# Pool mixer in column halves, another order of the conditioning weights, and copies and squares on ScalarE, in a two-layer diffusion backbone

## The chip, the cores and the metric

One core of one Trainium2 chip runs the kernel. The metric is the device time of one launch in microseconds (us); a time of a kernel is the median of its runs.

## What is computed

512 latent tokens and 256 context tokens of width 1024 go through two layers. Layer 0 mixes tokens by pooling, layer 1 by attention, and each is followed by a squared-ReLU MLP. Cut to what matters here:

```python
sh1, sc1, gt1, sh2, sc2, gt2 = ada_mods(c, w_ada[i], b_ada[i])   # silu(c) @ w_ada + b, six parts of 1024
h = modulate(rms_norm(x, g_mix_pre[i]), sh1, sc1)                # h * (1 + sc1) + sh1
# layer 0: four groups of 256 columns, windows 2, 4, 8, 16 over the tokens
diff_g = mean over window of h_g - h_g
y = concat_g(diff_g @ w_pool[g]) * pool_scale
x = x + gt1 * rms_norm(y, g_mix_post[i])
m = square(relu(modulate(rms_norm(x, g_mlp_pre[i]), sh2, sc2) @ w_mlp_in[i])) @ w_mlp_out[i]
x = x + gt2 * rms_norm(m, g_mlp_post[i])
# the context tokens take the same steps with the conditioning of c_ctx
```

`w_ada` has 4 MB for each of the six parts of a layer. The kernel loads it in chunks of 1 MB.

## The kernel before

Tokens are six tiles of 128 rows (t = 0 to 3 latents, 4 and 5 context), columns eight tiles of 128 (k = 0 to 7); pool group g holds k = 2g and 2g+1. Every product is made of three, from a rounded operand and its remainder (hH and hL of the activations, wpH and wpL of the pool weights): a cast on ScalarE makes the first, a subtraction on VectorE the second.

The stretch before the first MLP, which the change rewrites, has these parts:

- `rows_a`, `rows_b`: the rows come in, their mean squares go through GpSimd (`rstd`), and VectorE scales them into `acc`.
- `mean_mm(k)` (L420, tile psm): TensorE multiplies the rows by a band matrix, which gives window mean minus row for one k, in a PSUM tile of pool psA (two tiles of two banks each). `mean_ev` (L434) copies two of the eight into SBUF (tile stage); the others stay in PSUM until `centred`.
- `ada_mm` (L225, tile psada): one or two chunks of w_ada against the conditioning columns; VectorE turns the result (L227), four small products with `sel` finish the turn (L232), and `ada_out` adds the bias (L243) and makes scale and minus-shift columns (L252, L247). Chunks come in the order of the table `landing`: SC1 and SH1 for k 0 to 3 (two chunks each), SC1 and SH1 for k 4, 5 and for k 6, 7 (one chunk each), GT1 (four), then SC2 and SH2 in the same pieces.
- `centred(k)`: scale and shift of the mean (L452 on ScalarE, L454 on VectorE), cast (L455) and remainder (L456) into hH, hL.
- `pool_weights`: w_pool times pool_scale (L469), then its cast and remainder (L126, L129).
- `pool_a(t)` (L480, tile pspool): all four groups of one token tile, 24 matmuls into one psA tile. `pool_ms` takes the mean squares, `pool_b` (L325) multiplies by the gate rows, which `gate_rows` (L302, L304) spreads from GT1 in two column halves; `norm_r` (L328) adds to the residual, `norm_s` and `norm_c` (L512, L514) normalise for the MLP.
- `turn0`, `mod0`: transposes (L378, tile psx), scale and shift (L388, L390), cast and remainder (L394, L395). `Inner.part` (L553, tile psin) then multiplies by the first 256 columns of w_mlp_in, block by block.

After that comes the MLP of layer 0: `Inner` for its second 256 columns (96 matmuls on tile units), then fourteen rounds of `Seven` (Strassen-like products, L672) with `out_mm`, `out_ev` (L768 and L760 to L780) between them. VectorE also works off the conditioning of later parts there, one `ada_sum` (L263 to L272) for each call of `ada_step`, and builds the sums that `Seven` needs (`sums`, L617 to L620).

What sets the order: each step is put on a list with a number (`st.at`), and the list is run sorted. A scheduler then lays out each engine's instructions by its own estimate; only what is marked with `keep_in_program_order` keeps its place. Engines and the DMA queue of SyncE (SP) run their lists strictly in order. A load is issued when its buffer is free: w_ada and w_pool share the four buffers of pool `rawe`, pool_scale and the MLP weights the three of `rawp`. A buffer of a two-chunk unit is free after its matmuls for the first chunk, and after the `sel` products for the second, since the turned rows are put into it.

## Time and profile before

| | us |
|---|---|
| three runs | 1188.82, 1192.07, 1192.59 |
| median | 1192.07 |
| the profiled execution | 1189.55 |
| its span, first to last instruction | 1187.8 |
| around the span | 1.75 |
| TensorE (PE) busy in the span | 1147.0 |
| VectorE (DVE) | 950.5 |
| ScalarE (ACT) | 624.1 |

Starts in rows of the trace are microseconds from the start of the span. In a row of the timeline stand the start, the length of the merged run, engine, line, operation, tiles written and read, sizes, the count, and in brackets how long the engine sat idle before it and what ended that. A plain fp32 matmul (psm, psada, psg) counts twice, any other once. In a row by windows stand the window, its length, the busy time and number of instructions of PE, weight loads, DVE, ACT and POOL (GpSimd), TensorE's granted clock, the share of the DMA engines and GB/s.

### The profile page before, as it was taken

The page shows a single profiled execution, that of the slowest core. Times are in us where ns is not written, and L with a number is a line of the kernel's source. Part 1 is how long each engine was busy: PE and PEld are TensorE (multiplying, and loading weights), DVE is VectorE, ACT ScalarE, POOL GpSimd, SP SyncE. Part 2 cuts the span into 40 slices and gives each one's busy share as a digit, 9 for nine tenths or more (in the row PEclk, how much of TensorE's full clock was granted, in tenths as well). Part 3 has the DMA queues.
Part 4 walks back from the last instruction along what each step waited for, and adds up shares of the span by engine and source line. Part 5 has one row for each costly group of instructions (what it writes and reads, how often), then busy time and mean ns, then how long its engine had stood idle before and what let it go on. Part 6 is the DMA issues. An engine that isn't in the chain of part 4 may idle for free.

```text
span 1187.8 us, 15989 instructions
## 1 busy us (share of the span) xinstructions
PE 1147.0 (97%) x6170; PEld 990.3 (83%) x6170; DVE 950.5 (80%) x1564; ACT 624.1 (53%) x1063; POOL 67.7 (6%) x120
## 2 busy tenths in 40 slices
PE   5899999999999999999999999999899999999997
PEld 3679789989899889988887889998888888888886
DVE  3787968889889888986587689978687788778876
ACT  4666435443445444544576378872676346435522
POOL 2030000000000000000142210001100000000001
PEclk9899999999999999999999999999999999999999
DMA  9984134443444443333431301105344133314312
GB/s 338 363 292 178 36 107 142 142 142 107 144 136 146 142 142 95 130 131 107 179 105 36 107 1 36 37 4 195 122 141 154 46 120 133 113 39 142 107 33 109
DMA packets 100011, 147.84 MB, mean 124 GB/s; under 512 B 2736, under 2 KB 75872, under 8 KB 99936
## 3 DMA queue, kind: packets, MB, share of 16 engines
q1 hardware_dynamic: 99936, 146.84, 36.6%
q8 instruction: 48, 0.79, 0.3%
q14 instruction: 27, 0.22, 0.1%
HBM read 139.49 MB, written 7.34 MB: 124 GB/s over the span
## 4 chain that ended last, share of the span: by engine, by line
PE 47%; issue 33%; DVE 9%; ACT 5%; POOL 3%; DMA 2%; SPq 0%; POOLq 0%; DVEq 0%; ACTq 0%
PE pso L768 19%; PE psin L672 17%; PE po L1226 2%; PE psq L1015 2%; PE pss L1187 2%; POOL rs L169 1%; DVE rows L268 1%; PE psin L553 1%; DMA raw<-in_w_mlp_in 1%; POOL rs L1024 1%; ACT junk L154 1%; DVE sm L1191 1%; PE psada L225 1%; PE pspt L1212 1%; DVE units L129 1%
## 5 line engine op out<-in xcount | busy, mean ns | idle before, releaser
L768 PE MATMUL pso<-units,rb 128*128 128x512 f32 x1152 | 279.7, 394 | 4.0 <-ACT pso L760 2.9
L768 PEld LDWEIGHTS pso<-units,rb 128*128 128x128 f32 x1152 | 215.7, 189 | 47.9 <-ACT pso L760 3.6
L268 DVE SCALAR_TENSOR_TENSOR rows<-raw,cond,rows 128x256 f32<-128x256 f32 x280 | 122.0, 477 | 0.7
L780 DVE TENSOR_TENSOR acc<-acc,pso 128x512 f32<-128x512 f32 x135 | 88.5, 676 | 31.6 <-PE pso L768 31.3
L553 PE MATMUL psin<-ra,rb 128*128 128x512 f32 (+1 forms) x432 | 104.8, 342 | 2.4 <-ACT ra L363 1.6
L872 PE MATMUL pso<-units,pairs 128*128 128x512 f32 x336 | 82.3, 389 | 0.0
L553 PEld LDWEIGHTS psin<-ra,rb 128*128 128x128 f32 x432 | 70.3, 189 | 13.6 <-ACT ra L363 1.9
L553 PE MATMUL psin<-ra 128*128 128x512 f32 x256 | 80.6, 389 | 0.0
L872 PEld LDWEIGHTS pso<-units,pairs 128*128 128x128 f32 x336 | 63.1, 188 | 13.1
L876 DVE TENSOR_TENSOR acc<-acc,pso 128x512 f32<-128x512 f32 x72 | 48.6, 681 | 27.6 <-PE pso L872 27.6
L167 POOL TENSOR_SCALAR ms<-ss 128x1 f32<-128x1 f32 x20 | 11.4, 572 | 1010.5 <-ACT junk L154 998.8
L672 PE MATMUL psin<-ra,units 128*128 128x384 f32 x336 | 66.0, 338 | 0.7 <-ACT psin L684 0.6
L672 PE MATMUL psin<-sums,units 128*128 128x384 f32 x336 | 63.7, 337 | 0.3 <-ACT units L638 0.2
L672 PEld LDWEIGHTS psin<-ra,units 128*128 128x128 f32 x336 | 59.3, 188 | 4.2 <-ACT psin L684 0.9
L129 DVE TENSOR_TENSOR units<-raw,units 128x1024 fp32r<-128x1024 f32 (+2 forms) x49 | 55.2, 1151 | 7.3 <-ACT units L126 7.1
L672 PEld LDWEIGHTS psin<-sums,units 128*128 128x128 f32 x336 | 58.8, 188 | 2.4 <-ACT psin L680 0.7
L760 ACT COPY pso<-acc 128x512 f32<-128x512 f32 x42 | 24.3, 589 | 67.2 <-DVE acc L780 65.2
L553 PEld LDWEIGHTS psin<-ra 128*128 128x128 f32 x256 | 48.0, 188 | 10.0
L126 ACT CAST units<-raw 128x1024 fp32r<-128x1024 f32 (+2 forms) x49 | 47.2, 995 | 14.3 <-PE pso L768 10.3
L553 PE MATMUL psin<-rb 128*128 128x512 f32 (+1 forms) x144 | 52.7, 367 | 0.2 <-DVE rb L364 0.2
L1015 PE MATMUL psq<-units,ra 128*128 128x512 f32 x216 | 51.7, 392 | 0.0
L553 PE MATMUL psin<-rb,ra 128*128 128x512 f32 x128 | 49.8, 389 | 0.0
(253 smaller groups left out, 2350.2 us busy)
## 6 DMA issues: line engine op xcount, KB each, us to landing
raw<-in_w_ada SPq DMA_DIRECT2D x48, 1024.0 KB, 5.4
raw<-in_w_mlp_in SPq DMA_DIRECT2D x32, 1024.0 KB, 5.4
raw<-in_w_mlp_out SPq DMA_DIRECT2D x32, 1024.0 KB, 5.1
raw<-in_w_qkv SPq DMA_DIRECT2D x6, 1024.0 KB, 5.3
spill<-xr SPq DMA_DIRECT2D x10, 512.0 KB, 9.3
xr<-spill SPq DMA_DIRECT2D x10, 512.0 KB, 5.9
raw<-in_w_o SPq DMA_DIRECT2D x4, 1024.0 KB, 5.4
xr<-in_x SPq DMA_DIRECT2D x4, 512.0 KB, 4.4
```

Source lines behind the costliest of these rows:

```text
L126: a = sc.copy(hi, raw)
L129: b = ve.tensor_tensor(out=lo, in0=raw, in1=hi, op=ALU.subtract)
L268: ve.scalar_tensor_tensor(out=r, in0=raw[:, k, :], scalar=cond[:, k, c:c + 1], in1=r, op0=ALU.mult, op1=ALU.add)
L553: te.matmul(ps[:, bank, o:o + ln], w[:, k, fs], rhs, start=start, stop=(k == KT - 1 and n == 2), skip_group_check=len(ks) < KT)
L672: te.matmul(bank, w[k], a[k], start=start and k == 0 and m == 0, stop=stop and k == 3 and m == 2, skip_group_check=True)
L760: sc.copy(ps, accv[:, t, c0:c0 + w])
L768: te.matmul(pss[h][:, 0:cols[h][1]], a[:, f, ts_], w[:, f, cols[h][0]:sum(cols[h])], start=(n == 0 and not seeded[t]), stop=(n == len(seq) ...
L780: ve.tensor_tensor(out=d, in0=d, in1=ps[:, 0:w], op=ALU.add)
L872: te.matmul(ps, a, w, start=(m == 0), stop=(m == len(seq) - 1))
L876: ve.tensor_tensor(out=M[n][:, t], in0=M[n][:, t], in1=ps, op=ALU.add)
L1015: te.matmul(ps, a[:, k, sl], w[:, k % 4, :], start=(k == 0 and n == 0), stop=(k == KT - 1 and n == 2))
L1187: te.matmul(ps[:, c2, 0:384], a[:, sl], b[:, kv, 384 * c2:384 * c2 + 384], start=(n == 0), stop=(n == 2))
```

## The change

- **Means.** `mean_mm` runs for all eight k in a row, one every 1.3 units of the list, and `mean_ev` copies every one into SBUF; `centred` then works there in place.
- **Chunk order.** In `landing` GT1 now comes third of four: SC1, SH1 for k 0 to 5, then GT1, then SC1, SH1 for k 6, 7, then SC2, SH2. The first matmul of each chunk and the turn on VectorE are kept in the order of the list.
- **Pool weights.** Loaded behind the first four chunks, and pool_scale right behind them, now also in pool `rawe`; multiplied and split in two halves.
- **Pool mixer by halves.** `pool_mm(t0, g)` does two token tiles for one group; a psA tile now holds one column half of two token tiles. Its gate, mean square and product follow for each half.
- **Rows by feature pair.** `norm_c`, `turn0` and `mod0` keep the normalised rows of two token tiles side by side for each k.
- **ScalarE.** In `Inner.square` of layer 0 the square is made in place by ScalarE and cast by it, and VectorE makes only the remainder; eight of the twelve copies of the first `out_ev` go to ScalarE.
- **Later conditioning.** `ada_step` is left out once (at g = 1), and what is due at the end is finished in `before0`.

```diff
@@ ada_mm
-                te.matmul(ps[q:q + 32, 0:w * P], cond[:, at, :], raw[:, k, :], start=(at < 4), stop=(at >= 4))
+                mm = te.matmul(ps[q:q + 32, 0:w * P], cond[:, at, :], raw[:, k, :], start=(at < 4), stop=(at >= 4))
+                if k == 0:
+                    tc.keep_in_program_order(mm)
-        ve.transpose(rows, ps[:, 0:w * P])
+        tc.keep_in_program_order(ve.transpose(rows, ps[:, 0:w * P]))
@@ mean_ev, centred
+            d = stage[-1][:, TOK * (k % 2):TOK * (k % 2) + TOK]
+        for z, ps, f in zip(d, means[k], (sc.copy, ve.tensor_copy)):
+            f(z, ps[:, 0:z.shape[-1]])
...
-                sc.activation(z, pm[ci][:, 0:ln], AF.Identity, scale=sa, bias=b)
+                sc.activation(z, z, AF.Identity, scale=sa, bias=b)
@@ pool weights
-        pscale = rawp.tile([P, 2048], F32, tag="raw", name="pscale")[:, 0:D]
-        sy.dma_start(pscale, pool_scale[0].partition_broadcast(P))
+        pscale = pools[0].tile([P, 2048], F32, tag="raw", name="pscale")[:, 0:D]
+        tc.keep_in_program_order(sy.dma_start(pscale, pool_scale[0].partition_broadcast(P)))
@@ pool mixer
-    def pool_a(t):
-        pp_ = psA.tile([P, 2, 512], F32, tag="a", name="pspool")
...
+    def pool_mm(t0, g):
+        if (t0, g // 2) not in pooled:
+            pooled[t0, g // 2] = psA.tile([P, 2, 512], F32, tag="a", name="pspool")
...
+    def pool_b(t, h):
+        gated(t, accv[:, t, :], pooled[t - t % 2, h][:, t % 2, :], 512 * h, 512 * h + 512)
@@ Inner.square
+            if self.ntok == TOK:
+                sc.activation(r, r, AF.Square)
+                sc.copy(hi[:, f, :], r)
+                ve.tensor_tensor(out=lo[:, f, :], in0=r, in1=hi[:, f, :], op=ALU.subtract)
+                return
@@ the list
-    landing = ((21, SC1, 0, 4), (26.3, SH1, 0, 4), (29, SC1, 2, 2), (32, SH1, 2, 2), (39, SC1, 3, 2), (42, SH1, 3, 2),
-               (47.3, GT1, 0, 4), (52.6, GT1, 2, 4), (61, SC2, 0, 4), (66, SH2, 0, 4),
+    landing = ((21, SC1, 0, 4), (26.7, SH1, 0, 4), (33.7, SC1, 2, 2), (36.5, SH1, 2, 2),
+               (42, GT1, 0, 4), (47.7, GT1, 2, 4), (50.5, SC1, 3, 2), (53.3, SH1, 3, 2), (61.7, SC2, 0, 4), (67.3, SH2, 0, 4),
...
+        st.at(15 + 1.3 * k, mean_mm, k)
@@ out_ev, extra0
-                ve.tensor_copy(d, ps)
+                (ve.tensor_copy if c0 and t % 3 else sc.copy)(d, ps)
...
-        if g:
+        if g > 1:
             ada_step()
```

**TensorE, from the first chunk of SC1 to the turn of SH1.** Tile psm is the window means, six matmuls for each k; psada from raw and cond is a chunk (four matmuls of 512 columns), psada from raw and sel a turn. Before, the rows from the means of k 2 on:

```order
L225 MATMUL psada<-raw,cond 32x512 x4
L420 MATMUL psm<-gate,acc 128x136
L420 MATMUL psm<-gate,acc 128x144 x2
L420 MATMUL psm<-gate,acc 128x136 x4
L420 MATMUL psm<-gate,acc 128x144 x2
L420 MATMUL psm<-gate,acc 128x136 x4
L420 MATMUL psm<-gate,acc 128x144 x2
L420 MATMUL psm<-gate,acc 128x136 x3
L225 MATMUL psada<-raw,cond 32x512 x12
L232 MATMUL psada<-raw,sel 32x2x4 x8
```

One chunk stood ahead of the means of k 2, 3 and 4, the three others of SC1 and SH1 behind them, and both turns at once behind these. Now, with the means of k 2, 3 and 4 already ahead of the first row shown:

```order
L225 MATMUL psada<-raw,cond 32x512 x8
L420 MATMUL psm<-gate,acc 128x136
L420 MATMUL psm<-gate,acc 128x144 x2
L420 MATMUL psm<-gate,acc 128x136 x4
L420 MATMUL psm<-gate,acc 128x144 x2
L420 MATMUL psm<-gate,acc 128x136 x3
L234 MATMUL psada<-raw,sel 32x2x4 x4
L420 MATMUL psm<-gate,acc 128x136
L420 MATMUL psm<-gate,acc 128x144 x2
L420 MATMUL psm<-gate,acc 128x136 x3
L225 MATMUL psada<-raw,cond 32x512 x8
L234 MATMUL psada<-raw,sel 32x2x4 x4
```

The two chunks of SC1 now stand behind the means of k 2 to 4, the turn of SC1 behind those of k 5 and 6, and the chunks of SH1 behind all eight.

**VectorE, the same place.** Before, from the copies of the first two means to the first centred column:

```order
L434 COPY stage<-psm 128x256 x2
L227 STREAM_TRANSPOSE raw<-psada 128x512
L970 TENSOR_SCALAR grow<-grow 128x128
L227 STREAM_TRANSPOSE raw<-psada 128x512
L243 TENSOR_TENSOR mods_92<-psada,cols 128x8
L252 SCALAR_TENSOR_TENSOR avec_94<-mods_92,cols 128x8
L243 TENSOR_TENSOR mods_92<-psada,cols 128x8
L247 TENSOR_SCALAR phase<-mods_92 128x8
L454 TENSOR_SCALAR work<-stage,avec_94,mods_92 128x256 x2
```

The two turns (L227) and the two sums of the mods (L243) stood close together. Now:

```order
L229 STREAM_TRANSPOSE raw<-psada 128x512
L435 COPY stage<-psm 128x256
L245 TENSOR_TENSOR mods_92<-psada,cols 128x8
L254 SCALAR_TENSOR_TENSOR avec_94<-mods_92,cols 128x8
L435 COPY work<-psm 128x256 x2
L474 TENSOR_TENSOR raw<-raw,pscale 128x1024 x2
L229 STREAM_TRANSPOSE raw<-psada 128x512
L129 TENSOR_TENSOR rb<-raw,rb 128x1024
L245 TENSOR_TENSOR mods_92<-psada,cols 128x8
L129 TENSOR_TENSOR rb<-raw,rb 128x1024
L249 TENSOR_SCALAR phase<-mods_92 128x8
L454 TENSOR_SCALAR stage<-stage,avec_94,mods_92 128x256 x4
```

The pool weights times pool_scale (L474, both halves) now stand ahead of the turn of SH1 (the second L229), and the first half's remainder (L129) ahead of its mods (the second L245).

**TensorE, the pool mixer and the gates.** Tile pspool is the mixer, psg the gate rows. Before, from the first pool matmul to the turn of the second half of GT1:

```order
L480 MATMUL pspool<-rb,ra 128x256 x17
L232 MATMUL psada<-rows,sel 32x2x2 x4
L225 MATMUL psada<-raw,cond 32x512 x4
L480 MATMUL pspool<-rb,ra 128x256
L225 MATMUL psada<-raw,cond 32x512 x4
L480 MATMUL pspool<-rb,ra 128x256 x22
L232 MATMUL psada<-raw,sel 32x2x4 x4
L480 MATMUL pspool<-rb,ra 128x256 x8
L302 MATMUL psg<-ident,gc 128x128 x8
L225 MATMUL psada<-raw,cond 32x512 x8
L232 MATMUL psada<-raw,sel 32x2x4 x4
```

All SC1 and SH1 chunks stood ahead of this place. Now:

```order
L488 MATMUL pspool<-rb,ra 128x256 x35
L234 MATMUL psada<-rows,sel 32x2x2 x4
L225 MATMUL psada<-raw,cond 32x256 x8
L488 MATMUL pspool<-rb,ra 128x256 x13
L225 MATMUL psada<-raw,cond 32x512 x8
L234 MATMUL psada<-rows,sel 32x2x2 x4
L234 MATMUL psada<-raw,sel 32x2x4 x4
L304 MATMUL psg<-ident,gc 128x128 x8
L488 MATMUL pspool<-rb,ra 128x256 x12
L225 MATMUL psada<-raw,cond 32x512 x8
L488 MATMUL pspool<-rb,ra 128x256 x24
L234 MATMUL psada<-raw,sel 32x2x4 x4
```

48 pool matmuls (left half of t 4, 5, 0 and 1) now stand ahead of the gates, with the chunk of SH1 for k 4, 5 and those of GT1 between them; the chunks for k 6 and 7 have moved behind the row that ends this piece. Further down, the mixer's right half waits for these, and on VectorE all six residual sums (L330) now stand behind the last `centred`.

138 lines of the change are left out of this document (71 added, 67 removed).

## Prediction, made before the changed kernel had run

> **What bounds the kernel now.** I read the stages first (busy time by windows), then the timeline of each engine in the stretch before the first MLP.
>
> ```profile
> 20.00:30.00 10.00, 8.23 (x89) 5.96 (x90) 2.74 (x9) 1.29 (x2) 0.00 (x0) 0.96 1.03 353
> 60.00:70.00 10.00, 10.00 (x84) 8.18 (x88) 8.72 (x9) 5.54 (x12) 2.73 (x6) 1.00 0.90 318
> 130.00:150.00 20.00, 16.68 (x74) 13.04 (x72) 20.00 (x35) 7.69 (x10) 0.00 (x0) 1.00 0.00 1
> 200.00:300.00 100.00, 100.00 (x508) 90.04 (x507) 90.86 (x177) 48.15 (x73) 0.00 (x0) 1.00 0.39 125
> ...
> 59.97 2.02 PE L302 MATMUL psg<-ident,gc 128*128 128x128 f32 x16 [0.58 <-DVE gc L291]
> 82.96 0.58 PE L553 MATMUL psin<-ra,rb 128*128 128x256 f32 x2
> 109.61 16.81 PE L553 MATMUL psin<-ra,units 128*128 128x384 f32 x96
> ```
>
> Early on the DMA engines are full (share 1.03) and TensorE waits now and then; from 60 on TensorE is full. The first stretch ends at 109.61, where the 96 matmuls of the second `Inner` begin. Behind it TensorE waits in one place only, 130 to 150 us, where VectorE is busy 20.00 of 20.00 us; from 200 on it has no gap. The matmuls are the same in number and kind in both kernels, so a full TensorE takes from the change neither gain nor loss. The change is worth what it does to 109.61, and to the wait behind it.
>
> **Step 1, to the turn of SC1 and the chunks of SH1.**
>
> ```profile
> 17.98 0.91 DVE L434 COPY stage<-psm 128x256 f32<-128x256 f32 x2 [1.21 <-ACT stage L434]
> 19.46 5.12 PE L420 MATMUL psm<-gate,acc 128*128 128x136 f32 x36
> 24.51 2.78 PE L225 MATMUL psada<-raw,cond 128*32 128x512 f32 x24
> 27.11 0.22 PE L232 MATMUL psada<-raw,sel 128*32 128x8 f32 x8
> 35.65 1.68 PE L420 MATMUL psm<-gate,acc 128*128 128x136 f32 x12
> 28.45 0.17 DVE L243 TENSOR_TENSOR mods<-psada,cols 128x8 f32<-128x8 f32 x1
> ...
> raw<-in_w_ada SPq DMA_DIRECT2D x48, 1024.0 KB, 5.4
> ...
> xr<-in_x SPq DMA_DIRECT2D x4, 512.0 KB, 4.4
> ...
> pscale<-in_pool_scale SPq DMA_DIRECT2D x1, 512.0 KB, 9.9
> ```
>
> Now the means of k 2 to 4 come first. The one for k 2 needs the first copy out of PSUM, about 18.5; three take 5.12, so 23.6. The two chunks of SC1 take 2 x 0.93 (2.78 for three): 25.5. The means of k 5 and 6 take 3.4, the turn 0.2 (0.22 for two): 29.1. Only now is the buffer free into which pool_scale goes, since it shares the four of `rawe`. Its load then takes 4.4, as 512 KB of x do: 33.5. (In the old place it shows 9.9 behind other loads, but here only w_pool is ahead; 9.9 is the upper end.) TensorE meanwhile does k 7 and the chunks of SH1, to 32.7, against 27.3 before. On SP's queue the next chunks stand behind pool_scale and the buffers of SH1, so SC1 for k 4, 5 is issued near 32 and lands at 37.5 (5.4); TensorE asks for it after the turn of SH1, at 37, and for the others later still, so this costs nothing. It is paid only if those turns come earlier.
>
> The Trainium skill, page "DMA: Bandwidth & Descriptors", section "Anatomy of one DMA — SWDGE (gpsimd) path", gives a DMA about 2.0 us and its bytes over 436 GB/s, an estimate of 3.2 us here; the row's 4.4 decides, and by the page the sum would be 1.2 us less.
>
> **Step 2, the shift of k 0 to 3.**
>
> ```profile
> 36.96 2.28 DVE L469 TENSOR_TENSOR raw<-raw,pscale 128x2048 f32<-128x2048 f32 x1
> 27.36 0.72 DVE L227 STREAM_TRANSPOSE raw<-psada 128x512 f32<-128x512 f32 x1 [0.89 <-PE psada L232]
> 41.21 2.29 DVE L129 TENSOR_TENSOR rb<-raw,rb 128x2048 fp32r<-128x2048 f32 x1 [1.17 <-ACT rb L126]
> 28.71 1.52 ACT L452 ACTIVATE work<-stage,mods,avec 128x512 f32<-128x512 f32 x2 [10.28 <-DVE mods L243]
> 30.80 3.13 ACT L455 ACTIVATE ra<-work,phase 128x256 fp32r<-128x256 f32 x6
> 44.35 3.80 PE L480 MATMUL pspool<-rb,ra 128*128 128x256 f32 x17 [0.18 <-DVE work L454]
> 62.91 6.01 PE L480 MATMUL pspool<-rb,ra 128*128 128x256 f32 x48
> ```
>
> VectorE runs in order, and the product with pool_scale stands ahead of the turn of SH1. So 33.5 + 2.28 + 0.72 for the turn + 1.14 for half a remainder + 0.2 = 37.8 for the mods of SH1, which were there at 28.6. ScalarE then does four L452 (3.0) and eight L455 (0.52 each, 4.2): 45.0. All of them now read SBUF in place of PSUM; the row shown (stage) does so already. The pool matmuls start after the first column, near 42.2; the first 17 took 3.80 after a pause, the other 18 take 2.25: 48.2. Before, they began at 44.35, held by the pool weights, so up to here little is lost.
>
> **Step 3, the gates.**
>
> ```profile
> 54.50 1.95 PE L302 MATMUL psg<-ident,gc 128*128 128x128 f32 x16
> 56.25 0.58 ACT L304 COPY gate<-psg 128x512 f32<-128x512 f32 x1
> L325 DVE TENSOR_TENSOR acc<-pspool,gate 128x512 f32<-128x512 f32 x12 | 7.7, 680 | 4.6 <-ACT gate L304 2.8 <-ACT junk L154 1.6
> ```
>
> TensorE next does a turn, the SH1 chunk, 13 pool matmuls, two chunks of GT1 and a turn (0.25 + 0.93 + 1.6 + 1.9 + 0.25): 53.1. Then it stands still: the turn of GT1 is behind three remainders of k 4 and 5 on VectorE, these behind ScalarE's L452 (1.5) and three L455 (1.6), these behind the mods that came at 53.3. So 56.5, remainder and turn 1.3, sel and gate columns 0.5: 58.3. Half the gate matmuls 1.0, a copy 0.58, two products of 0.68: 61.2. Only then is a psA tile free, because two halves of finished mixer (t 4, 5 and t 0, 1) hold both until their gate is there. A whole tile was held so before, too, but with the chunks for k 6 and 7 already done.
>
> **Step 4, the right half.** From 61.2 TensorE does 12 pool matmuls, two chunks and 24 pool matmuls (1.5 + 1.9 + 3.0): 67.6; turn and gate columns 0.7, gates 2.0, 12 pool matmuls 1.5: 71.8. Then SC1 for k 6, 7: chunk 0.93, transpose 0.44, turn 0.3, and the same for SH1: 75.1. Mods 0.3, two L452 and four L455 (1.5 + 2.1), the last remainder 0.5: 79.5. The first token tile's last matmuls take about 0.9: 80.4.
>
> ```profile
> 63.21 2.47 DVE L328 SCALAR_TENSOR_TENSOR xr<-acc,rs,xr 128x1024 f32<-128x1024 f32 x2
> L154 ACT ACTIVATE junk<-pspool 128x512 bf16<-128x512 f32 x12 | 7.1, 595 | 3.5 <-PE pspool L480 3.4
> 56.12 0.56 POOL L169 TENSOR_TENSOR rs<-ms,nhalf 128x1 f32<-128x1 f32 x1
> L328 DVE SCALAR_TENSOR_TENSOR xr<-acc,rs,xr 128x1024 f32<-128x1024 f32 x6 | 7.6, 1275 | 0.3
> L390 DVE TENSOR_SCALAR acc<-psx,avec,mods 128x256 f32<-128x256 f32 x12 | 6.1, 537 | 4.9 <-ACT acc L388 4.9
> L395 DVE TENSOR_TENSOR ra<-acc,ra 128x512 fp32r<-128x512 f32 x12 | 7.8, 687 | 1.0 <-ACT ra L394 1.0
> L514 DVE TENSOR_SCALAR acc<-xr,rs 128x1024 f32<-128x1024 f32 x3 | 2.3, 751 | 1.5 <-POOL rs L169 1.5
> ```
>
> Mean square 0.6, then GpSimd's two steps at 0.56 at most: the first residual sum at 82.1, where it was at 63.21. That is the heart of it: k 6 and 7 are due in the right half of all six tiles, and their chunks now come after the gates.
>
> **Step 5, VectorE's pile.** Between the first gated right half and the first remainder of the MLP's input, VectorE now has in one row six products (6 x 0.68), six residual sums (6 x 1.275), four quarters of w_mlp_in's remainder (4 x 0.69, as L395), three turns (0.72 each at most), three `norm_c` (3 x 0.75), three scalings (3 x 0.54) and five small ones (0.17 each): 21.3. The strided write of `norm_c` is not in the trace; at the price of the residual sum, 1.275, it adds 1.6, and less than 0.75 nothing suggests; I take 0.75, the same engine and size. From 81.0 that gives 102.3, and one wait for GpSimd 1.0: the first psin matmul at 103.3, against 82.96. Behind that the old kernel took 26.65 to 109.61, with 32 transposes among it; now 24 are left, eight at no more than a pool matmul (0.125) less: 25.6. **The stretch ends at 128.9, 19.3 later.**
>
> **Step 6, given back behind it.**
>
> ```profile
> 149.48 5.12 PE L768 MATMUL pso<-units,rb 128*128 128x512 f32 x13 [0.89 <-ACT pso L760]
> 133.85 11.08 PE L768 MATMUL pso<-units,rb 128*128 128x512 f32 x48
> L573 DVE TENSOR_TENSOR work<-work 128x768 f32<-128x768 f32 x1 | 1.0, 957 | 1.0 <-ACT work L560 1.0
> L268 DVE SCALAR_TENSOR_TENSOR rows<-raw,cond,rows 128x256 f32<-128x256 f32 x280 | 122.0, 477 | 0.7
> ```
>
> TensorE waited 3.3 there (16.68 busy of 20.00), the last of it for seeds that ScalarE copies once VectorE has copied `acc`; and its next 13 matmuls took 5.12 where 48 take 11.08, which is 2.1 more than their share (3.0). VectorE loses four squares of 0.96, eight copies (0.68, as L325 for the same size out of PSUM) and one `ada_step` (14 x 0.48): 16 us of what filled it. ScalarE, busy 7.69 of 20, takes the squares' four casts and the copies. Both gaps should mostly go; I take 4.0 of 5.4. The six more seeded sums later (ScalarE for VectorE) lie beside a full TensorE.
>
> **The sum.** The profiled execution took 1189.55 (span 1187.8), 2.5 below the median of the three runs. 1189.55 + 19.3 - 4.0 = **1204.9**.
>
> **Rivals.**
> - **TensorE stays full** from the gates on: then the stretch ends at 61.2 + (109.61 - 59.97) + four more chunks than were left then (3.7) = 114.5, the gap behind it goes whole, and the time is 1189.55 + 4.9 - 5.4 = 1189. For it speaks that 60 to 110 was full before; against, that the residual chains of all tiles now begin together. 0.10.
> - **Faster:** the stalls of steps 1 to 3 do not arise, since pool_scale lands before the rows of SH1 and the gates come as the left halves end. The matmuls of 61.2 then start at 50, the stretch ends at 103.3, and the time is 1178. It decides where that start lies before 58. Against it stands VectorE's order. 0.08.
> - **Slow restarts.** TensorE's rows after a pause are slow, and its granted clock is low in them:
>
> ```profile
> 31.53 3.06 PE L420 MATMUL psm<-gate,acc 128*128 128x136 f32 x12 [1.10 <-DVE work L454]
> 32.00:34.00 2.00, 2.00 (x10) 2.00 (x10) 2.00 (x5) 2.00 (x5) 0.00 (x0) 0.50 1.09 355
> ```
>
> One mean took 3.06 at a clock of 0.50, where 35.65 shows 1.68: 1.4 lost. Of the new pauses (33 to 38, 53 to 58, 75 to 79) step 2 has the first in its 3.80 for 17; the other two would add 2.8, and the time is 1207. 0.12. The Trainium skill, page "TensorE: Matmul & The Clock Gate", section "Part 1: The HAM clock gate (the "warmup" mystery)", has the clock halved after an idle window of about 3.4 us until one such window was busy, so up to 1.7 us a pause, an estimate of 3.4 for two and 1208 in all; the 0.50 agrees.
> - **Nothing given back:** ScalarE becomes late with the copies that it takes over, and TensorE waits for it in VectorE's place: 1208.9. 0.08.
>
> **Chances.** Forecast 0.62, with 1193 to 1212 as its own range: half of step 5 hidden beside TensorE at the lower end (11.5 less), pool_scale at 9.9 and `norm_c` at 1.275 at the upper (7.1 more). The range is 1190 to 1214; outside lie the faster case, half of the full TensorE and a little above, near 0.19. A measurement of this kernel tells about 0.3%, 3.6 us, from no change. Faster: 0.08 + 0.03 of the full case = 0.11. Same: 0.07 + 0.05 from the forecast's lower end = 0.12. Slower: 0.77.
>
> **What would show it.** Right: pool_scale issued near 29 and VectorE idle until it lands; the mods of SH1 near 38; TensorE idle from 53 to 58 and 75 to 79; the first residual sum near 82; the 96 matmuls at about 129; no gap of TensorE after it. Wrong: the first residual before 75, or psin starting before 95 with TensorE full.

## The result, and the profile after

The changed kernel took **1205.7 us** (median of 4 runs, 1203.99 to 1206.49) against 1191.59 for the kernel before, run beside it (median of 4, 1188.82 to 1192.59): a ratio of **1.012, 95% interval 1.010 to 1.014**, 14.1 us slower. The forecast was 1204.9. Its profiled execution took 1203.99, with a span of 1202.3 (before: 1189.55 and 1187.8).

The stages of the changed kernel first. The columns are those of the windows shown in the prediction: length, busy time of TensorE, of its weight loads, of VectorE, ScalarE and GpSimd (instructions in brackets), TensorE's granted clock, share of the DMA engines, GB/s.

```profile
30.00:40.00 10.00, 5.56 (x52) 2.49 (x51) 7.48 (x15) 5.08 (x7) 0.00 (x0) 0.77 0.78 262
50.00:60.00 10.00, 4.61 (x47) 3.13 (x46) 4.17 (x12) 6.16 (x14) 0.00 (x0) 0.79 0.72 238
80.00:90.00 10.00, 7.03 (x38) 6.63 (x41) 6.74 (x9) 5.36 (x13) 4.48 (x8) 0.67 0.17 66
140.00:150.00 10.00, 10.00 (x58) 9.74 (x57) 10.00 (x16) 5.19 (x7) 0.00 (x0) 1.00 0.33 106
```

TensorE is idle 4.4 us of the 10 from 30, 5.4 of the 10 from 50, and 3.0 of the 10 from 80, and its clock is below 0.8 in all three. The old hole at 140 to 150, where TensorE was busy 6.68 of 10, is closed. Where TensorE stood still, and for whom, its timeline tells (start, duration, operation, and in brackets the idle time before it and its releaser):

```profile
29.61 0.25 PE L234 MATMUL psada<-raw,sel 128*32 128x8 f32 x8
...
36.67 0.30 PE L234 MATMUL psada<-raw,sel 128*32 128x8 f32 x8 [3.34 <-DVE raw L229]
...
41.89 6.08 PE L488 MATMUL pspool<-rb,ra 128*128 128x256 f32 x35 [2.02 <-ACT ra L455]
...
57.36 0.29 PE L234 MATMUL psada<-raw,sel 128*32 128x8 f32 x8 [4.68 <-DVE raw L229]
58.36 3.75 PE L304 MATMUL psg<-ident,gc 128*128 128x128 f32 x16 [0.70 <-DVE gc L293]
62.49 1.76 PE L488 MATMUL pspool<-rb,ra 128*128 128x256 f32 x12 [0.38 <-DVE acc L327]
...
66.04 3.13 PE L488 MATMUL pspool<-rb,ra 128*128 128x256 f32 x24
...
79.18 4.92 PE L488 MATMUL pspool<-rb,ra 128*128 128x256 f32 x24 [2.23 <-ACT ra L455]
87.07 2.90 PE L488 MATMUL pspool<-rb,ra 128*128 128x256 f32 x12 [2.97 <-DVE acc L327]
...
107.25 4.56 PE L562 MATMUL psin<-ra,rb 128*128 128x256 f32 x36
...
131.88 16.81 PE L562 MATMUL psin<-ra,units 128*128 128x384 f32 x96
```

Two long waits are for a turn of conditioning rows on VectorE (36.67, 57.36), one for ScalarE's shift of k 6 and 7 (79.18). One more, which the prediction does not have, is for VectorE's gate products (87.07), after which a psA tile is free again; the 12 matmuls behind it are slow (2.90, where 12 others took 1.69). The 96 matmuls of the second `Inner` begin at 131.88, 22.3 later than the 109.61 of before, and no row behind them in this stretch waits. VectorE's timeline at the places that the prediction names:

```profile
33.63 2.36 DVE L474 TENSOR_TENSOR raw<-raw,pscale 128x1024 f32<-128x1024 f32 x2 [1.08 <-DMA pscale<-in_pool_scale]
35.91 0.71 DVE L229 STREAM_TRANSPOSE raw<-psada 128x512 f32<-128x512 f32 x1
...
37.64 0.16 DVE L245 TENSOR_TENSOR mods<-psada,cols 128x8 f32<-128x8 f32 x1
...
79.16 2.42 DVE L456 SCALAR_TENSOR_TENSOR ra<-work,mods,ra 128x256 fp32r<-128x256 f32 x4 [1.14 <-ACT ra L455]
...
83.99 0.69 DVE L327 TENSOR_TENSOR acc<-pspool,gate 128x512 f32<-128x512 f32 x1 [2.41 <-ACT junk L154]
85.04 1.28 DVE L330 SCALAR_TENSOR_TENSOR xr<-acc,rs,xr 128x1024 f32<-128x1024 f32 x1 [0.36 <-POOL rs L169]
```

The product with pool_scale waits 1.08 for its load and stands ahead of the turn of SH1; the first residual sum comes at 85.04 (63.21 before).

So the loss is 22.3 us up to the 96 matmuls, and 7.8 come back behind them: from there to the end of the span it takes 1202.3 - 131.88 = 1070.4, where it took 1187.8 - 109.61 = 1078.2. This split is used for every run below. "From the turn" counts from the matmuls that turn SC1 on TensorE (29.61 above) to the 96, since runs of one and the same beginning reach that turn up to 3 us apart; where the edit moves the turn itself, the column is empty. The changed kernel was measured once, beside a kernel before of 1191.59. The kernel before was measured again with each later group of runs and gave 1190.0 to 1191.06, so a time "below the changed kernel" is good to some 1.5 us only.

| kernel | time, us | 96 matmuls at | from the turn | behind them |
|---|---|---|---|---|
| before | 1190.0 to 1191.6 | 109.61 | 82.5 | 1078.2 |
| changed | 1205.70 | 131.88 | 102.3 | 1070.4 |
| e1 late edits alone | 1179.36 | 109.34 | 81.0 | 1068.8 |
| e11 squares alone | 1186.72 | 107.97 | 82.7 | 1076.3 |
| e2 changed, no late edits | 1214.41 | 135.82 | 105.6 | 1080.2 |
| e3 gates last | 1205.19 | 132.42 | 102.3 | 1070.7 |
| e8 gates last, chunk close | 1198.12 | 124.08 | 94.8 | 1070.8 |
| e4 product behind the turn | 1200.55 | 129.14 | 99.5 | 1069.3 |
| e7 and means late | 1200.13 | 129.13 | | 1068.9 |
| e9 old order and loads | 1199.36 | 128.61 | 97.7 | 1069.0 |
| e6 split early | 1204.85 | 133.89 | 103.8 | 1068.9 |
| e5 long fill | 1205.19 | 133.79 | 103.5 | 1069.2 |
| e10 short fill | 1203.41 | 131.68 | 100.8 | 1070.3 |
| e12 e1 and means first | 1188.85 | 116.62 | | 1070.2 |

### The profile page after: what moved, and what is told of

The parts are those of the page before. It is cut to its first block, busy times and chain, and to the rows that moved or that the text cites. A ratio compares the mean times of both kernels' runs of the same rounds, so it can differ in the third digit from the quotient of the medians.

```text
span 1202.3 us, 16005 instructions
## 1 busy us (share of the span) xinstructions
PE 1150.0 (96%) x6170; PEld 996.8 (83%) x6170; DVE 945.1 (79%) x1557; ACT 642.2 (53%) x1097; POOL 68.3 (6%) x120
## 4 chain that ended last, share of the span: by engine, by line
PE 53%; issue 32%; DVE 6%; ACT 4%; POOL 3%; DMA 2%; SPq 0%; POOLq 0%; DVEq 0%; ACTq 0%
PE pso L785 21%; PE psin L686 17%; PE psin L562 3%; PE po L1246 2%; PE psq L1032 2%; PE pspool L488 2%; PE pss L1207 1%; PE psada L225 1%; POOL rs L169 1%; PE psm L420 1%; ACT junk L154 1%; POOL rs L1041 1%; DVE sm L1211 1%; PE pspt L1232 1%; DVE rows L270 1%
## 5 line engine op out<-in xcount | busy, mean ns | idle before, releaser
L270 DVE SCALAR_TENSOR_TENSOR rows<-raw,cond,rows 128x256 f32<-128x256 f32 x280 | 127.9, 483 | 2.0
L129 DVE TENSOR_TENSOR units<-raw,units 128x1024 fp32r<-128x1024 f32 (+2 forms) x49 | 55.4, 1157 | 6.5 <-ACT units L126 6.3
L795 ACT COPY acc<-pso 128x512 f32<-128x512 f32 x48 | 27.1, 587 | 43.7 <-PE pso L785 43.0
```

Source lines behind the costliest of these rows:

```text
L129: b = ve.tensor_tensor(out=lo, in0=raw, in1=hi, op=ALU.subtract)
L270: ve.scalar_tensor_tensor(out=r, in0=raw[:, k, :], scalar=cond[:, k, c:c + 1], in1=r, op0=ALU.mult, op1=ALU.add)
L795: sc.copy(d, ps)
```

## The experiments

"Late edits" are the change's three edits behind the front: four squares and most of the first evictions go to ScalarE, and one `ada_step` is left out.

**e1, the late edits on the kernel before.**

```diff
+            if self.ntok == TOK:
+                sc.activation(r, r, AF.Square)
+                sc.copy(hi[:, f, :], r)
+                ve.tensor_tensor(out=lo[:, f, :], in0=r, in1=hi[:, f, :], op=ALU.subtract)
+                return
...
-                ve.tensor_copy(d, ps)
+                (ve.tensor_copy if c0 and t % 3 else sc.copy)(d, ps)
...
-        if g:
+        if g > 1:
             ada_step()
...
```

> The kernel before with only the late edits of the change: four squares of the first MLP's widest Inner and the first evictions of the output sums to ScalarE, and the ada_step of g = 1 left out (its last piece finished before block 0 closes). Of the 22.3 us that the changed kernel loses up to the 96 matmuls, 8.3 come back by the end. Theory: these edits give them back, because VectorE is the engine that TensorE waits for between 130 and 150 us (and at 432 us); then they do so without the new front as well, no gap of TensorE is left between 130 and 160, and the time is 1183 (1181 to 1186) against 1191.6. Rival: the longer front gives them back, because weights are loaded and split while TensorE waits; then this kernel gains at most the stop at 432 us, and the time is 1188 to 1192.

Measured: 1179.36, ratio 0.990 (0.988 to 0.992), 10.7 us **faster than before**, and more than the theory had. Its window where the old kernel's VectorE was full and TensorE waited:

```profile
140.00:150.00 10.00, 10.00 (x51) 8.93 (x50) 4.01 (x5) 5.05 (x9) 0.00 (x0) 1.00 0.11 45
```

VectorE falls to 4.01 of 10.00 and TensorE is full. Matmuls of the same place in TensorE's order come 6.2 us sooner than in the kernel before at its 192 us (185.44 for 191.61), and at the end 9.7 sooner (spans of 1178.1 and 1187.8). Part of the second gain is at a stop that the prediction did not see. In the kernel before, TensorE's timeline from 200 to 500 us has two waits:

```profile
432.78 0.73 PE L768 MATMUL pso<-units,rb 128*128 128x512 f32 x2 [0.68 <-ACT units L126]
433.73 0.62 PE L672 MATMUL psin<-sums,units 128*128 128x384 f32 x2 [0.21 <-ACT units L638]
```

In e1 and in the changed kernel there is none up to 500; behind that each has two short ones before 660 (0.43 and 0.65), as the kernel before has (0.61 and 0.65). The two waits make 0.89 of the 3.5 between; where the rest comes from is not shown. The rival (the longer front gives the time back) falls: here the front is the old one.

**e2, the changed kernel without them** (the diff of e1 backwards).

> The changed kernel with those late edits taken back (squares and evictions on VectorE, ada_step at g = 1). Theory: the stretch up to the 96 matmuls still ends near 131.9, the stop of TensorE behind it is there again, and the time is 1214 (1211 to 1216). Rival, the longer front gives the time back: 1205 to 1208, with no stop behind the 96 matmuls.

Measured: 1214.41, ratio 1.020 (1.018 to 1.023). TensorE's timeline behind the 96:

```profile
171.60 0.73 PE L780 MATMUL pso<-units,rb 128*128 128x512 f32 x2 [0.46 <-ACT units L126]
174.38 0.50 PE L780 MATMUL pso<-units,rb 128*128 128x512 f32 x1 [2.04 <-ACT pso L772]
175.76 5.04 PE L780 MATMUL pso<-units,rb 128*128 128x512 f32 x13 [0.89 <-ACT pso L772]
```

These are the waits of the kernel before (0.46, 1.97, 0.89), here as 0.46, 2.04, 0.89: nothing is given back. The expected start at 131.9 was missed by 3.9, in a front that ran slower in this profile (clock 0.51 from 40 to 50, 0.72 in the changed kernel), and the profiled execution was the slowest of the four (1217.83; the others 1213.65 to 1215.10). The front of the other three was not seen; behind the 96 the verdict is plain, 1080.2.

**e11, the squares alone** on the kernel before (the first five added lines of e1).

> The kernel before with one of the three late edits alone: the four squares of the first MLP's widest Inner go to ScalarE. All three together gave 10.7 us, 6 of them between 126 and 180 us and some 3.5 near 432 and 560 us. Theory: the four squares are 3.8 us of VectorE's work in the stretch in which TensorE waits for it, so they give about that much there and nothing later: 1187.5 (1186 to 1189). Rival: the eight evictions that VectorE keeps are what fills it, and the squares give nothing: 1190 to 1192. Second rival: a small relief is enough, since the stop is a wait for seeds behind VectorE's copies, and the squares give all 6 us: 1184 to 1186.

Measured: 1186.72 (8 runs), ratio 0.997 (0.996 to 0.998), as the theory had it. Of the three waits (0.46, 1.97, 0.89) two are left, of 0.46 and 1.16, and the stop near 430 stays:

```profile
143.74 0.73 PE L773 MATMUL pso<-units,rb 128*128 128x512 f32 x2 [0.46 <-ACT units L126]
145.63 0.97 PE L677 MATMUL psin<-sums,units 128*128 128x384 f32 x4 [1.16 <-ACT units L643]
...
427.33 0.73 PE L773 MATMUL pso<-units,rb 128*128 128x512 f32 x2 [0.68 <-ACT units L126]
```

By the times 3.8 of the 10.7 us come from the squares. The profile has 1.9 of that behind the 96 (1076.3 for 1078.2), and 1.6 ahead of them, where the edit changes nothing. So the squares give 2 to 4, and the evictions and the `ada_step` together the rest; these two were not parted.

**e3, gates last.** The changed kernel with SC1 and SH1 for k 6, 7 ahead of GT1, and what needs a gate due behind it.

```diff
-               (42, GT1, 0, 4), (47.7, GT1, 2, 4), (50.5, SC1, 3, 2), (53.3, SH1, 3, 2), (61.7, SC2, 0, 4), (67.3, SH2, 0, 4),
+               (39.3, SC1, 3, 2), (42.1, SH1, 3, 2), (47.7, GT1, 0, 4), (53.3, GT1, 2, 4), (61.7, SC2, 0, 4), (67.3, SH2, 0, 4),
...
```

> The changed kernel with the conditioning chunks in the old order: SC1 and SH1 for k 6, 7 ahead of both halves of GT1, with the steps that need a gate due behind it. Theory (step 4: the right half waits for k 6 and 7, and these for chunks that come after the gates): the shift of k 6, 7 is done near 61 and not 81.6, the first residual sum starts near 75 and not 85, VectorE's row of work of some 22 us follows from there, the 96 matmuls start near 122, and the time is 1196 (1193 to 1199). Rival: the stops of TensorE at 33 to 42 and 53 to 58 are the cause, and the later gates add to them, since the left halves hold both psA tiles for longer: 1205 to 1210. Second rival: the row of work on VectorE runs as long from wherever it starts and something else sets its start: 1204 to 1207.

Measured: 1205.19, ratio 1.012 (1.010 to 1.014): **no gain, and the theory failed.** VectorE's timeline:

```profile
64.16 0.71 DVE L456 SCALAR_TENSOR_TENSOR ra<-work,mods,ra 128x512 fp32r<-128x512 f32 x1
...
83.86 0.69 DVE L327 TENSOR_TENSOR acc<-pspool,gate 128x512 f32<-128x512 f32 x1 [1.79 <-ACT gate L306]
84.65 1.28 DVE L330 SCALAR_TENSOR_TENSOR xr<-acc,rs,xr 128x1024 f32<-128x1024 f32 x1
```

The last remainder of k 7 is done at 64.9, 16.7 sooner than in the changed kernel. But the product of the right half now waits for a gate copy (83.86 `<-ACT gate`), since the chunk for that gate stands behind 60 pool matmuls on TensorE, and the residual sum comes at 84.65, where it came at 85.04 in the changed kernel. The second rival had the size right: something else set the start.

**e8, gates last with the second chunk close.** The same, with that chunk directly behind the first gates, and the pool matmuls that follow due a little later. The diff is against e3.

```diff
-               (39.3, SC1, 3, 2), (42.1, SH1, 3, 2), (47.7, GT1, 0, 4), (53.3, GT1, 2, 4), (61.7, SC2, 0, 4), (67.3, SH2, 0, 4),
+               (39.3, SC1, 3, 2), (42.1, SH1, 3, 2), (47.7, GT1, 0, 4), (50.2, GT1, 2, 4), (61.7, SC2, 0, 4), (67.3, SH2, 0, 4),
...
```

> The kernel with the conditioning chunks in the old order, in which the first residual sum came at 84.65 although k 6, 7 were shifted at 64.9, with one more edit: the chunk of the second half of GT1 directly behind the gates of the first half, so that it no longer stands behind 60 pool matmuls on TensorE. Theory: the right half waits for the later of two, its gates and k 6, 7, and in that kernel the gates of the right half (copies at 83.2) were the later; they now come near 77, the first residual sum near 79.5, and the time is 1200 (1198 to 1202). Rival: the two psA tiles hold the row of pool matmuls whatever comes first, and the time stays 1204 to 1206.

Measured: 1198.12, ratio 1.006 (1.004 to 1.008), 7.6 below the changed kernel; in the theory's range.

```profile
75.84 0.69 DVE L327 TENSOR_TENSOR acc<-pspool,gate 128x512 f32<-128x512 f32 x1 [1.76 <-ACT gate L306]
76.64 1.28 DVE L330 SCALAR_TENSOR_TENSOR xr<-acc,rs,xr 128x1024 f32<-128x1024 f32 x1
```

The right half's product at 75.84 and the residual sum at 76.64 are earlier than expected (79.5 for the sum), 8.4 sooner than in the changed kernel, and the 96 matmuls come 7.8 sooner with them. The right half waits for the later of two, its gate (as here and in e3) and the shift of k 6, 7 (as in the changed kernel, where its gates were there at 72.6); moving one alone (e3) shows nothing.

**e4, the product behind the turn.** Pinned so that the turn and mods of SH1 come first on VectorE.

```diff
-        st.at(34 + 2 * h, pool_weights, h)
+        st.at(32 + 0.5 * h, pool_weights, h)
...
-        ve.tensor_tensor(out=w4, in0=w4, in1=pscale[:, 512 * h:512 * h + 512].rearrange("p (g n) -> p g n", n=256)
+        tc.keep_in_program_order(ve.tensor_tensor(out=w4, in0=w4, in1=pscale[:, 512 * h:512 * h + 512].rearrange("p (g n) -> p g n", n=256)
```

> The changed kernel with the product by pool_scale pinned behind the turn of SH1 on VectorE (step 2). Theory: the mods of SH1 come near 35 and not 37.6, the first pool matmuls are then held by the pool weights and by ScalarE's shift of k 0 to 3 until near 41, the 35 end some 1.5 us sooner, and that is what the time gains: 1204 (1202 to 1206). Rival, the product ahead of the turn is what starts the whole delay: the gates and all behind them come 3 us or more sooner, 1200 to 1203. Other side: the remainders of the pool weights come so late that the pool matmuls start later than 41.9, and the time is 1206 to 1209.

Measured: 1200.55, ratio 1.009 (1.007 to 1.011), 5.1 below the changed kernel (3.6, if each is taken against the kernel before that was measured beside it), in the rival's range and not in the theory's.

```profile
34.47 0.17 DVE L245 TENSOR_TENSOR mods<-psada,cols 128x8 f32<-128x8 f32 x1 [0.37 <-PE psada L234]
```

```profile
38.08 1.94 PE L225 MATMUL psada<-raw,cond 128*32 128x256 f32 x16 [3.68 <-DMA raw<-in_w_ada]
...
56.91 2.02 PE L304 MATMUL psg<-ident,gc 128*128 128x128 f32 x16 [0.75 <-DVE gc L293]
```

The mods come at 34.47 (37.64). The time so won meets the load of the next chunk (TensorE waits 3.68 for it, as step 1 had said it would once the turn came earlier), so the pool matmuls start later, at 44.45 for 41.89, as the third case of the expectation feared. The time fell all the same: the gates come 1.45 sooner, and their matmuls take 2.02 for 3.75, behind a wait of 0.84 in place of 4.68.

**e7, and the means of k 5 to 7 late.** e4, with these means pinned behind the chunks of SC1 and SH1.

```diff
-        st.at(15 + 1.3 * k, mean_mm, k)
-        st.at(16.4 + 1.3 * k, mean_ev, k)
+        z = 1.3 * k + (7 if k > 4 else 0)
+        st.at(15 + z, mean_mm, k)
+        st.at(16.4 + z, mean_ev, k)
...
+                if k > 4 and q == i == 0:
+                    tc.keep_in_program_order(mm)
```

> The kernel with the product by pool_scale behind the turn of SH1, and now also the means of k 5 to 7 pinned behind the chunks and turns of SC1 and SH1 on TensorE (step 1). Theory: the mods of SH1 come near 31 (34.5 without it, 37.6 in the changed kernel), the shift of k 0 to 3 ends near 38, pool matmuls run from 39, both gates and all behind them come some 4 us sooner than with the product moved alone, the stretch ends near 125, and the time is 1196.5 (1194.5 to 1198.5). Rival: the loads of the next conditioning chunks, which wait for buffers, hold TensorE instead: 1199 to 1202, with TensorE waiting for DMA ahead of the chunks of k 4, 5.

Measured: 1200.13, ratio 1.008 (1.006 to 1.010), what e4 gives, no more.

```profile
30.90 0.17 DVE L245 TENSOR_TENSOR mods<-psada,cols 128x8 f32<-128x8 f32 x1 [0.37 <-PE psada L234]
```

```profile
38.21 2.25 PE L420 MATMUL psm<-gate,acc 128*128 128x136 f32 x12 [4.35 <-DVE stage L437]
40.40 1.94 PE L225 MATMUL psada<-raw,cond 128*32 128x256 f32 x16
```

The mods of SH1 are at 30.90, as expected. But now the mean of k 7 waits 4.35 for a PSUM tile that VectorE copies out behind four remainders and half of the product with pool_scale, and the next conditioning chunk stands behind it on TensorE until 40.40. One wait went, its neighbour took its place; it was not the rival's wait for a load either.

**e9, old order and old loads.** The changed kernel with the due times of before for the conditioning chunks, and w_pool and pool_scale loaded behind the chunks of k 4, 5.

```diff
-    landing = ((21, SC1, 0, 4), (26.7, SH1, 0, 4), (33.7, SC1, 2, 2), (36.5, SH1, 2, 2),
-               (42, GT1, 0, 4), (47.7, GT1, 2, 4), (50.5, SC1, 3, 2), (53.3, SH1, 3, 2), (61.7, SC2, 0, 4), (67.3, SH2, 0, 4),
+    landing = ((21, SC1, 0, 4), (26.7, SH1, 0, 4), (29, SC1, 2, 2), (32, SH1, 2, 2),
+               (39, SC1, 3, 2), (42, SH1, 3, 2), (47.3, GT1, 0, 4), (52.6, GT1, 2, 4), (61.7, SC2, 0, 4), (67.3, SH2, 0, 4),
...
-    st.at(30, pool_load)
...
+    st.at(33.5, pool_load)
...
```

> The changed kernel with the conditioning steps at their old due times (SC1 and SH1 for k 4 to 7 ahead of the gates) and with w_pool and pool_scale loaded behind the chunks of k 4, 5, as in the kernel before. Theory, loads: from 20 to 60 us the DMA engines' shares sum to 4.20 before and to 3.01 in the changed kernel, some 12 us of transfers less, because w_pool and pool_scale hold two of the four buffers from 26 us and the chunks behind them on SP's queue start at 32.5 and not at 28.4; with the old order the share returns to near 1.0, the pool matmuls start near 43, the first residual sum comes near 67 and not 85, the 96 matmuls near 114, and the time is 1186 (1184 to 1190). Rival, work: the long chain is that of VectorE and ScalarE over the eight means, copied out of PSUM first, and does not care for the loads; the first residual sum stays behind 72 and the time is 1192 to 1197.

Measured: 1199.36, ratio 1.008 (1.006 to 1.010): above the rival's range, far above the theory's.

```profile
30.00:40.00 10.00, 5.77 (x69) 3.32 (x67) 4.54 (x14) 5.31 (x10) 0.00 (x0) 0.92 0.94 299
50.00:60.00 10.00, 9.86 (x98) 7.51 (x94) 5.93 (x17) 6.66 (x15) 0.00 (x0) 0.90 1.04 373
```

```profile
40.31 0.29 PE L234 MATMUL psada<-rows,sel 128*32 128x4 f32 x8 [3.70 <-DVE rows L229]
...
63.80 0.29 PE L234 MATMUL psada<-raw,sel 128*32 128x8 f32 x8 [3.94 <-DVE raw L229]
```

The DMA share is back at 0.94 and 1.04 (0.78 and 0.72 in the changed kernel), and the 96 matmuls come only 3.3 sooner, at 128.61 and not near 114: TensorE waits 3.70 and 3.94 for VectorE's turns, which stand in order behind remainders that wait for ScalarE. Loads alone are not the cause.

**e12, means first.** e1 with all eight means first and copied out of PSUM, pool_scale in the weights' buffers, all else as before.

```diff
-        st.at([15, 16, 18, 20, 22, 29.5, 31, 35][k], mean_mm, k, k in (4, 7))
-        if k < 2:
-            st.at(16.5 + k, mean_ev, k, (True, False))
+        st.at(15 + 1.3 * k, mean_mm, k)
+        st.at(16.4 + 1.3 * k, mean_ev, k)
...
-        pscale = rawp.tile([P, 2048], F32, tag="raw", name="pscale")[:, 0:D]
+        pscale = pools[0].tile([P, 2048], F32, tag="raw", name="pscale")[:, 0:D]
...
```

> The kernel before with the three late edits (1179.4 without the following) and one more part of the change alone: all eight means come first on TensorE and are copied out of PSUM into SBUF, with pool_scale in the buffers of the weights as in the changed kernel. The column halves, the order of the conditioning chunks and gates and the loads stay as before. Theory, means first: it is what is left of the loss in the kernel with the old loads (the 96 matmuls at 128.6 there, 109.6 before), since it holds the chunks of SH1 and its turn back by some 5 us and puts copies of 8 x 0.58 and 8 x 0.42 on ScalarE and VectorE ahead of the shift; the mods of SH1 come near 33 and not 28.6, the first gates near 59 and not 54.5, the 96 matmuls near 114, and the time is 1184 (1182 to 1187). Rival, the column halves: the means are ready long before the pool weights, which start the pool matmuls near 44 in either kernel, so nothing comes later than before, and the time is 1178 to 1181; then what the halves do, two psA tiles held until the gates and all six right halves behind them, is the rest of the loss.

Measured: 1188.85 (10 runs), ratio 0.999 (0.998 to 1.000), 9.5 above e1: this part alone nearly uses up what the late edits give.

```profile
42.16 1.94 PE L225 MATMUL psada<-raw,cond 128*32 128x256 f32 x16 [4.46 <-DMA raw<-in_w_ada]
...
65.08 0.25 PE L232 MATMUL psada<-raw,sel 128*32 128x8 f32 x8 [3.87 <-DVE raw L227]
```

The loss is larger than the theory had (116.62, not 114, and a time above its 1182 to 1187), and the rival falls. TensorE waits 4.46 for a chunk that is loaded behind pool_scale, and 3.87 for a turn; how much is the means' and how much pool_scale's place, this run does not part.

**e6, the weights' split early.** The changed kernel with the four quarter splits of w_mlp_in due before the shift of k 6, 7.

```diff
-        st.at(61 + 1.5 * q, lambda q: split(*raws[0], True, q), q)
+        st.at(55.1 + 0.1 * q, lambda q: split(*raws[0], False, q), q)
```

> The changed kernel with the four quarter splits of the first w_mlp_in weights due ahead of the shift of k 6, 7, where VectorE and ScalarE wait, and not among the residual sums. Theory (step 5: VectorE's row of work from the first gated right half sets the start of psin): 2.7 us leave that row, psin starts near 104.5 and not 107.25, and the time is 1203 (1201.5 to 1204.5). Rival: the chain from ScalarE's mean squares over GpSimd to the residual sums sets it, and VectorE's waits grow by what its work loses: 1205 to 1207.

Measured: 1204.85, ratio 1.012 (1.010 to 1.013), the rival's. VectorE's timeline in the row of residual sums:

```profile
91.58 1.28 DVE L330 SCALAR_TENSOR_TENSOR xr<-acc,rs,xr 128x1024 f32<-128x1024 f32 x1 [1.21 <-POOL rs L169]
...
99.05 0.69 DVE L327 TENSOR_TENSOR acc<-pspool,gate 128x512 f32<-128x512 f32 x1 [1.16 <-ACT junk L154]
```

2.7 us of work left the row, and waits for GpSimd and ScalarE took its place (1.21 ahead of the third sum, 0.66 in the changed kernel; 1.16 ahead of a product). From the first residual sum to the first psin it is 22.5, against 22.2. The row itself starts 1.3 later (86.36), since the early remainders now stand ahead of the turn for the second gates, so the time alone would not tell the two apart.

**e5 and e10, pauses filled.** The changed kernel with added matmuls into a PSUM tile that nobody reads, behind the shift values of k 4, 5 and of k 6, 7: 34 and 16 in e5, 15 and 8 in e10.

```diff
+    def warm(n, src):
+        ps = psB.tile([P, 512], F32, tag="b", name="warm")
+        for _ in range(n):
+            te.matmul(ps[0:2, 0:P], src, ident, start=True, stop=True)
...
+    st.at(43.05, warm, 34, mods[0][:, SH1 * KT + 4:SH1 * KT + 6, 0])
+    st.at(54.35, warm, 16, mods[0][:, SH1 * KT + 6:SH1 * KT + 8, 0])
```

> The changed kernel with 50 added matmuls of 128 x 128 into a PSUM tile that nobody reads, in two of TensorE's pauses: 34 once the shift values of k 4, 5 are there (pause from 52.7 to 57.4) and 16 once those of k 6, 7 are there (76.9 to 79.2). Theory, slow restarts: the 16 gate matmuls behind the first pause took 3.75 against 2.02 for the next 16, and 24 pool matmuls behind the second took 4.92 against 3.13, so with the pauses filled both return to about 2.0 and 3.1, the third block of pool matmuls starts some 1.7 us sooner, the stretch ends near 128.5 to 130, and the time is 1203 (1201.5 to 1204.5). Rival: the rows are long because their operands come late, and the fill changes nothing: 1205 to 1207.

> As the kernel with the filled pauses, whose 50 added matmuls turned out as 100 rows of 0.11 us and held the turn of GT1 back by some 3 us: now 15 and 8 (30 and 16 rows, 3.6 and 1.9 us), which end before the turns that they stand ahead of. Theory: the gate matmuls take 2.05 and the 24 pool matmuls 3.13, as they did there, and now nothing is held back, so the first residual sum comes near 82.5 and not 85.0, the 96 matmuls near 129.3, and the time is 1203 (1201 to 1204.5). Rival: the time so won is lost again in the row of work on VectorE, and the time stays 1205 to 1207.

Measured: 1205.19 for e5, ratio 1.012 (1.010 to 1.013), and 1203.41 for e10, ratio 1.011 (1.009 to 1.013). TensorE's timelines, e5 and then e10:

```profile
54.01 6.60 PE L465 MATMUL warm<-ident,mods 128*2 128x128 f32 x59 [0.31 <-DVE mods L245]
...
61.59 2.05 PE L304 MATMUL psg<-ident,gc 128*128 128x128 f32 x16
```

```profile
60.31 2.02 PE L304 MATMUL psg<-ident,gc 128*128 128x128 f32 x16 [0.75 <-DVE gc L293]
...
80.06 3.81 PE L493 MATMUL pspool<-rb,ra 128*128 128x256 f32 x24
```

and the window from 57 to 60, in which the gate matmuls begin, in the changed kernel and then in e10 (where they begin at 60.31 and the fill lies in it):

```profile
57.00:60.00 3.00, 1.94 (x16) 1.87 (x17) 1.25 (x5) 0.00 (x0) 0.00 (x0) 0.50 0.30 93
```

```profile
57.00:60.00 3.00, 1.63 (x21) 1.01 (x18) 2.84 (x6) 1.47 (x3) 0.00 (x0) 1.00 0.51 167
```

The 16 gate matmuls take 3.75 behind a clock of 0.50, and 2.02 to 2.05 behind one of 1.00 with the pause filled: that slow restarts make this row long is shown. The Trainium skill, page "TensorE: Matmul & The Clock Gate", section "Part 1: The HAM clock gate (the "warmup" mystery)", halves the clock after some 3.4 us without work until as long a window was busy; behind the pause of 4.68 that would cost up to 1.7, an estimate, and 1.73 was measured. The trace agrees there, and not behind the shorter waits of the last section.

The second fill parts two causes. The 24 pool matmuls behind the shift of k 6, 7 took 4.92 in the changed kernel, at a clock of 0.50 from 80 to 83. In e10 they took 3.81 at a clock of 1.00, begun as VectorE began the four remainders (80.06 and 80.04); in e5 3.13, begun 1.7 behind it (83.10 and 81.36). So some 1.1 of the 1.8 goes with the clock, and some 0.7 with operands that come late, as the rival had it. In e5 the fill came out as 100 rows, twice what I had counted, and held the turn back. In e10 the 96 matmuls come 1.5 sooner from the turn and the time is 2.3 lower (1.2 against the kernel before beside each); the intervals overlap, so the time alone does not settle it. The pause ahead of 87 us stayed open, and in e10 the chunk behind it took 3.53, for 1.95 in the changed kernel, which hides part of the gain.

## Why the prediction was right, step by step

The time (1204.9 forecast, 1205.7 measured) is right, and the two parts that make it are each 3 to 4 us off, in opposite directions: the front lost 22.3 and not 19.3, and 7.8 and not 4.0 came back. That the two errors cancel is luck.

- **Step 1, right, partly by luck.** The product started at 33.63 (33.5), since the issue came 0.8 later than forecast and the load took 0.8 less, 3.6 for the 4.4 of the x rows; the two errors cancel (the changed kernel's table of DMA issues; the last column is the us from issue to landing):

```profile
pscale<-in_pool_scale SPq DMA_DIRECT2D x1, 512.0 KB, 3.6
```

  The Trainium skill's estimate (page "DMA: Bandwidth & Descriptors", section "Anatomy of one DMA — SWDGE (gpsimd) path"), 3.2, was the nearer of the two, though that section is on DMAs that GpSimd issues, and this load was issued on SyncE's queue.
- **Step 2, right in its times, too cheap.** The mods of SH1 at 37.64 to 37.80 (37.8), the shift of k 0 to 3 done at 44.9 (45.0), the first 35 pool matmuls at 48.0 (48.2). "Little is lost" was wrong: the product ahead of the turn costs about 4 to 5 us in all (e4), though the pool matmuls start 2.6 later without it.
- **Step 3, right but for the clock.** TensorE waited from 52.7 to 57.4 and had its gate values at 58.36 (53.1 to 58.3). The gate matmuls then took 3.75 where the sum had 2.0, and the third block started at 62.49 (61.2).
- **Step 4, the times right, the cause half right.** Shift of k 6, 7 done at 81.6 (79.5), first residual sum at 85.04 (82.1); the slow rows ahead of that sum are of the size of the 2.9: 1.7 in the gates, 1.8 in 24 pool matmuls (4.92 at 79.18, 3.13 at 66.04), of the latter only some 1.1 by the clock (e10). "The heart of it" holds only together with the gates: k 6, 7 alone moved nothing (e3), both together 7.6 us (e8).
- **Step 5, the size right, the mechanism not.** From the first right product to the first psin 23.3 (22.3), and on to the 96 in 24.6 (25.6). But it is not VectorE's pile that sets it: 2.7 us out of it change nothing (e6). The waits that took its place in e6 point to the chain mean square on ScalarE, two steps on GpSimd, residual sum, for six tiles at once; no run shortens that chain, so this is argued and not shown.
- **Step 6, too small.** Forecast 4.0, measured 7.8. The wait at 130 to 150 and its slow rows gave 5.9 by 208 us: the last row here and 191.61 before are the same matmul in TensorE's order, 16.4 apart and no longer 22.3.

```profile
207.98 2.27 PE L686 MATMUL psin<-ra,units 128*128 128x384 f32 x12
```

```profile
191.61 2.27 PE L672 MATMUL psin<-ra,units 128*128 128x384 f32 x12
```

  The rest comes later, in part at the stop at 432 us: the prediction had said that TensorE has no gap from 200 on.
- **The rivals.** "Slow restarts" was no rival but came on top: priced at 2.8 (which makes 1207.7, not the 1207 it gives) and given 0.12, it made the rows long as it said, and the stretch ended 3.0 later than the 128.9 forecast. Its pauses were not all: the one ahead of 87 us cost 1.2 more. Filling two pauses gave 1.5 back (e10). That TensorE stays full, or that the stalls do not arise, is refuted by the rows above; that nothing is given back, by e1.

What the 22.3 us consist of is settled in part only: order of chunks and gates 7.8 at the 96 matmuls (e8), product ahead of the turn 2.7 (e4), slow restarts about 1.5 (e10), means first with pool_scale's place 7.3 on the old order (e12, 116.62 against 109.34). They were measured on different kernels, overlap (e4 shortens the pause ahead of the gates, which e10 fills), and need not add up. Of the 22.3, 2.5 stand already at the turn of SC1 (29.61 for 27.11), where step 1 had 29.1 and where runs of one beginning differ by as much. The column halves alone were not tried.

The version that beats both is e1: the kernel before with the late edits only, 1179.36, 26.3 us below the changed kernel.

## What to carry to other kernels

Split a large change at the place where its parts stop touching each other, and measure both sides: here one half of it lost 22 us and the other gained 8 to 10, and only the sum was seen. Where an instruction needs two things, moving one shows nothing; look at the releaser of the row in the new trace before giving up the idea. A short instruction that other engines wait for (here a 0.7 us turn) must not stand in order behind one that waits for a load or for another engine. And relieving the engine that is full while TensorE waits for it paid at once, in either front.

## What the runs showed of the hardware

- Three runs with the same instructions up to there reach the turn of SC1 at different times: 25.23 in e11, 27.11 before, 28.37 in e1. A single profile's front is good to some 3 us only; the medians are steadier.
- The clock also fell without a long pause: in the changed kernel TensorE was busy 2.19 of the 5 us from 75 to 80 at a clock of 0.98, and the next 5 us were granted 0.68, behind a wait of 2.23. Behind the wait of 2.97 it was 0.50 from 87 to 90.

```profile
75.00:80.00 5.00, 2.19 (x35) 1.29 (x36) 2.46 (x9) 2.79 (x5) 0.00 (x0) 0.98 0.87 290
80.00:85.00 5.00, 4.10 (x22) 3.89 (x21) 2.27 (x4) 1.72 (x5) 0.85 (x2) 0.68 0.34 129
```

- How long the low clock lasts differs at the same place: behind the row at 87 us it was 0.97 from 89.9 to 91.8 in the changed kernel, and 0.53 from 89.7 to 93.2 in e10.
